# Order of VectorE's sums in the MLP chunks, and activation parts in halves at a layer's last down chunk, in a one-core fp32 encoder trunk

## The chip, the core and the metric

The kernel runs on one core of a Trainium2 chip. TensorE (PE in the profile, PEld for its weight loads) multiplies, VectorE (DVE) and ScalarE (ACT) make its operands and empty its banks, GpSimd (POOL) and SyncE (SP) issue DMAs. The metric is the device time of one execution in microseconds (us). Three runs of the kernel before gave 1590.45 to 1590.70 us, median 1590.61.

## The reference, cut to what matters

Two request groups of 512 and 256 tokens go through two layers, 768 tokens side by side in the kernel. The part that the change touches is the MLP that ends each layer's mixer:

```python
h = rms_norm(x, norm_mlp[i])
x = x + jnp.square(jax.nn.relu(h @ mlp_w_up[i])) @ mlp_w_down[i]     # 1024 -> 4096 -> 1024
gate = jax.nn.sigmoid(rms_norm(x, norm_ple[i]) @ ple_w_gate[i])
x = x + (p[i] @ ple_w_proj[i]) * gate
```

All of it is fp32.

## The kernel before, in words

**A product in three matmuls.** An fp32 value is split into a high part that TensorE takes at its faster fp32 rate (`hi`, written by an ACT copy) and the rest (`lo = value - hi`, a DVE subtraction, in some places a POOL DMA that adds). A product is hi·hi + hi·lo + lo·hi, so TensorE needs the `hi` part of a weight first and its `lo` part some matmuls later. `split` is `high` and then `low`.

**Seven products for eight.** Both MLP matrices are multiplied by a Strassen-Winograd scheme: a chunk of weights and of activations is cut in 2 x 2 blocks, and seven products of sums of blocks replace eight. The weight sums are made on the fly on DVE: `sums32` (line 479 and 480) gives the blocks s3 and s2, `sums14` (lines 484 and 485) gives s1 and s4. The activation sums are `t13` and `t42` (lines 408 to 414), and their high and low parts are written at lines 418 and 424; the parts of the activation blocks that enter directly are written at lines 450 and 454 (high) and 460 and 463 (low). All matmuls are issued at line 180.

**Jobs.** Each layer's MLP has 16 up chunks (u = 0 to 15; the first two are done plainly, without the scheme) and 8 groups of two down chunks. After the plain ones the order is: up 2g+2, down (g, 0), down (g, 1), up 2g+3, for g = 0 to 6, and then the last group's two down chunks, `down_first` and `down_last`. A job has seven products of 12 matmuls of 384 columns each. An even up chunk is thus followed by a down chunk; an odd one by an even up chunk or, for u = 15, called `final`, by `down_first`.

**What sets the order.** In this stage the instruction streams of ACT, PE and DVE run as the program writes them; each engine takes its instructions strictly in that order and waits at the first that isn't ready. While TensorE does one job, ACT and DVE prepare the weights of the next job (`v`, a `Weights7`), finish the job before (`pend`, a list of steps of which `late()` takes the next), and read the banks.

**An up chunk** (`up`, line 1355 on) issues for TensorE: w11 into bank `a`; s3 into `b`; s2 onto `a`; w12 onto `c`; s1 onto `a`; w22 onto `d`; s4 onto `a`. In between ACT copies `a` to `c` (line 1366), `b` to `p` (1373) and `a` to `d` (1378). The sum `a + p` is taken by DVE at line 1389, when s1 is done, and s4 may write `a` only after it has been read. On DVE there follow the rectified block from `c` (line 1146), the low part of the next direct weights (`wlo`, line 532), a `late()` step, the low part of s32 (`zlo`), `d + p` (line 1405, when w22 is done), and the rectified rest. Ahead of line 1389 DVE does `sums32`, `sums14` and one `late()` step (a `t` low part, line 424).

**A down chunk** begins with w11 into two banks `a`, then s3 into two banks of tag `B`, which has two banks in all: the second of them is the one that held the up chunk's `d`.

**The layer's end.** The last group's activations of u = 15 can't be prepared during other up or down chunks: they are needed at once. `up` with `final` prepares block x11; `down_first` waits for the rest: after its first product, ACT squares y2 (768 columns, line 1149), writes the high part of x21 and x22 (line 454), then copies both banks `a` to `C` (line 1452), then squares the rest of y1 (line 1518). `t13`, `t42` and the parts follow, 768 columns each. The last product block of u = 15 enters each of the w12 and s3 products late (`late=True`: first the matmuls with u = 14's activations). Then come the high and low parts of the sum weights s14 (`whi<-sum`, `wlo<-sum`).

Of the kernel before, what the change touches and what calls it, by code (L numbers as in the profile page):

```python
# [11 lines left out]
F32 = mybir.dt.float32  # L12
F32R = mybir.dt.float32r
AF = mybir.ActivationFunctionType
ALU = mybir.AluOpType
# [7 lines left out]
T = sum(SEQS)  # L23
# [14 lines left out]
H = T // 2  # L38
# [10 lines left out]
def trunk_kernel(ctx: ExitStack, tc: tile.TileContext, a: dict, out: bass.AP):  # L49
    nc = tc.nc  # L50
    act, dve, pe = nc.scalar, nc.vector, nc.tensor
# [75 lines left out]
    def bank(tag, name):  # L127
        pool = pair_of_banks if tag == "B" else psum
        return pool.tile([P, 512], F32, tag=tag, name=name, bufs=BANKS[tag])
# [72 lines left out]
    def slot(i, name, dt=F32R, n=T):  # L202

        return (slots if i < 32 else more).tile([P, n], dt, tag=f"S{i}", name=name)

    def big(name, dt=F32):

        nonlocal turn
        if more is None:
            return tmp.tile([P, T], dt, tag="t", name=name)  # L210
        turn += 1
        return tmp.tile([P, T], dt, tag=f"q{turn % 6}", name=name, bufs=1)
# [12 lines left out]
    class Norm:  # L225


        n = T
# [166 lines left out]
    class Sums:  # L395
# [30 lines left out]
        def added(self, i):  # L426

            hi, lo = self.t[i]
            act.activation(lo[:], hi[:].bitcast(F32), AF.Copy, scale=-1.0)
            nc.gpsimd.dma_start(lo[:], (self.q1, self.q2)[i][:], accum_op=ALU.add)  # L430
# [11 lines left out]
    class Acts(Sums):  # L442
# [14 lines left out]
        def lowx(self, i):  # L457
            if i == 0:
                hi, lo = self.x1
                dve.tensor_tensor(lo, self.q1[:, :H], hi.bitcast(F32), ALU.subtract)  # L460
            else:
                hi, lo = self.x2
                dve.tensor_tensor(lo[:], self.q2[:], hi[:].bitcast(F32), ALU.subtract)  # L463

    class Weights7:

# [80 lines left out]
    def product7(ps, w, key, xs, start, step=P, col=0):  # L547

        hi, lo = w.w[key]
        rhs = xs[QS7[key]]  # L550
        ks = [(slice(step * i + col, step * i + col + P), rhs[i]) for i in range(512 // step)]
        terms = [(hi[:, c], p) for c, ps_ in ks for p in ps_] + [(lo[:, c], ps_[0]) for c, ps_ in ks]
        for i, (a, b) in enumerate(terms):
            matmul(ps, a, b, start=start and i == 0, stop=i == len(terms) - 1, skip_group_check=True)
# [581 lines left out]
    def mlp(l, norm, nxt, w, places, early, product=None, begun=None, more_gates=()):  # L1136
# [8 lines left out]
        def rectified(t, src, o, e, op):  # L1145
            dve.scalar_tensor_tensor(t[:, o:e], src, 0.0, r[:, o:e], op, ALU.mult)

        def squared(t):
            act.activation(t[:], t[:], AF.Square)  # L1149

        def acts_of(u, y1, y2, rest):

            e = chunk_acts(u, y1, y2)
            return [
                lambda: squared(rest),
                lambda: e.highx(0),
                lambda: (e.highx(1), e.lowx(0), e.lowx(1), e.t13()),
                e.t42,
                lambda: e.high(0),
                lambda: e.high(1),  # L1160
                lambda: e.low(0),
                lambda: e.low(1),
            ]

        def chunk_acts(u, y1, y2):
            return Acts(y1, y2, places[7 * (u % 2) : 7 * (u % 2) + 7], groups[u // 2], u % 2)

        def late(n=1):

            for _ in range(n):  # L1170
                if pend:
                    pend.pop(0)()
# [182 lines left out]
        def up(u, w, make):  # L1355


            first, final = u == PLAIN[l], u == 2 * NG - 1
            w.low("s32")
            w.split("s14")  # L1360
            v = make()
            seven = isinstance(v, Weights7)
            a = bank("A", "a")[:, :H]
            product7(a, w, "w11", xs, True)
            c = bank("A" if first else "C", "c")[:, :H]
            act.activation(c, a, AF.Copy)
            late(len(pend) - 5)
            w.split("w22")
            late()
            b = bank("A" if first else "B", "b")[:, :H]  # L1370
            product7(b, w, "s3", xs, True)
            p = big("p")[:, :H]
            act.activation(p, b, AF.Copy)
            if seven:
                v.sums32()
            product7(a, w, "s2", xs, False)
            d = bank("B", "d")[:, :H]
            act.activation(d, a, AF.Copy)
            late(2)
            if seven:  # L1380
                v.sums14()
                (v.sum_added if final else lambda: v.high("s32"))()
            late()
            product7(c, w, "w12", xs, False)
            if seven:
                v.high("direct")
            product7(a, w, "s1", xs, False)
            y1, y2 = big("y1"), big("y2")
            dve.tensor_tensor(y2[:, H:], a, p, ALU.add)  # L1389
            rectified(y1, c, 0, H, ALU.max)  # L1390
            if final:
                e = chunk_acts(u, y1, y2)
                act.activation(y1[:, :H], y1[:, :H], AF.Square)
                e.highx(0)
            if seven:
                v.low("direct")
            late()
            if seven:
                v.low("s32")
            if final:  # L1400
                e.lowx(0)
            product7(d, w, "w22", xs, False)
            if seven:
                v.added("w22")
            dve.tensor_tensor(y2[:, :H], d, p, ALU.add)
            rectified(y2, y2[:], 0, T, ALU.min)
            if final:
                squared(y2)
                e.highx(1)
            product7(a, w, "s4", xs, False)  # L1410
            rectified(y1, a, H, T, ALU.max)
            if final:
                aside.append(e)
            else:
                pend.extend([lambda: squared(y2)] + acts_of(u, y1, y2, y1))
            return v

        def down(g, h, w, make):
# [58 lines left out]
            if end:  # L1477
                return (down_first, down_last)[h](w, before or make, top, low, products, copies, added, third, less)
# [31 lines left out]
        def down_first(w, make, top, low, products, copies, added, third, less):  # L1510


            e = aside.pop()
            a = [bank("A", "a")[:, :H] for _ in range(2)]
            products(a, "w11", True)
            e.lowx(1)
            c = copies("C", a)
            act.activation(e.q1[:, H:], e.q1[:, H:], AF.Square)
            e.t13()
            e.high(0)  # L1520
            e.t42()
            products(c, "w12", False, True)
            e.low(0)
            e.high(1)
            e.low(1)
            w.split("s14")
            v = make()
            p = third()
            added(top, 0, c, ALU.add)
            products(a, "s2", False)  # L1530
            d = copies("B", a)
            v.sums32()
            v.high("direct")
            v.sums14()
            v.high("s32")
            products(a, "s1", False)
            added(low, H, a, ALU.subtract)
            v.low("direct")
            products(d, "w22", False)
            v.added("w22")  # L1540
            added(low, 0, d, ALU.subtract)
            products(a, "s4", False)

            def rest():
                added(top, H, a, ALU.add)
                v.low("s32")
                v.low("s14")
                less(p)

            return v, (lambda: v.high("s14"), rest)  # L1550
# [69 lines left out]
        with tc.manual_schedule(engines={ET.Activation, ET.PE, ET.DVE}):  # L1620
            for i, (job, *args) in enumerate(jobs):

                def make():

                    what, *n = jobs[i + 1]
                    if what is not down:
                        return up_chunk(l, *n)
                    k = (KB // 2) * n[0] + 2 * n[1]
                    return Weights7(a_down[k], a_down[k + 1])

                a_down = a["down"][l]
                w = job(*args, w, make)
# [557 lines left out]
    others = [i for i in rest + old if i not in parts]  # L2190
# [120 lines left out]
```

## Time and profile before

| what | value |
|---|---|
| median of three runs | 1590.61 us (1590.45 to 1590.70) |
| profiled execution, its own time | 1591.22 us |
| its span, first to last instruction | 1589.4 us |
| granted TensorE clock, mean | 0.994 |
| MLP of layer 0 and of layer 1, in the span | about 290 to 748 us and 1042 to 1505 us |
| time from an even chunk's s4 to the next one's | 55.55 to 55.57 us |

A row of the timeline gives the start, the duration, the engine, the line, the operation, the tile written and those read, the shapes and the count of instructions merged into it; in square brackets, how long the engine was idle before it and what released it. Two DVE instructions overlap a little: the second starts before the recorded end of the first.

### The profile page before, as it was taken

To read this page: it belongs to the slowest core of one execution; us is meant where nothing else is said; L and a number is where in the kernel's file an instruction comes from. 1 tells how busy PE (TensorE), PEld (TensorE's weight loads), DVE (VectorE), ACT (ScalarE), POOL (GpSimd) and SP (SyncE) were. 2 spreads that over 40 slices of the span, in tenths; PEclk is the share of its full clock that TensorE was granted. 3 is DMA by queue.
4 is the path that set the end of the run, shared out by engine and by line. 5 is a ranking of instruction groups with operands and counts; after the bars stand their busy time and mean duration, and the time that the engine had idled before them with its cause. 6 is when DMAs were issued, how large, how long until landed. Compare 5 with 4: busy or idle time off the path is not lost.

```text
span 1589.4 us, 24597 instructions
## 1 busy us (share of the span) xinstructions
PE 1543.9 (97%) x9375; PEld 1489.7 (94%) x9375; DVE 1357.7 (85%) x2244; ACT 982.2 (62%) x1566; POOL 151.0 (9%) x172
## 2 busy tenths in 40 slices
PE   9999999999999999999989999999999999999996
PEld 7988889999999999999989999999999999999885
DVE  7599898898889889889898887869888988988986
ACT  7478766876566656667755344556656665665754
POOL 0211000011111111110000000000111111111000
PEclk9999999999999999999999999999999999999998
DMA  8854412445654644556522212122564554456522
GB/s 278 216 135 134 132 52 91 128 100 129 137 120 120 140 115 105 129 137 152 147 60 80 80 67 85 63 78 69 138 137 114 128 139 102 108 137 140 138 78 103
DMA packets 72694, 188.39 MB, mean 119 GB/s; under 512 B 8144, under 2 KB 26064, under 8 KB 72576
## 3 DMA queue, kind: packets, MB, share of 16 engines
q1 hardware_dynamic: 45440, 139.89, 28.3%
q0 software_dynamic: 27136, 46.93, 16.7%
q8 instruction: 73, 1.20, 0.3%
q14 instruction: 45, 0.37, 0.1%
HBM read 143.02 MB, written 10.48 MB: 97 GB/s over the span
## 4 chain that ended last, share of the span: by engine, by line
PE 61%; DVE 22%; ACT 10%; issue 4%; DMA 4%; SPq 0%; DVEq 0%; ACTq 0%
PE a L180 28%; PE mm L180 7%; PE b L180 6%; PE B L180 4%; PE C L180 4%; PE c L180 3%; PE d L180 2%; DVE t L424 2%; PE pt L847 1%; ACT y L1149 1%; PE gate L180 1%; PE p L180 1%; DVE act L463 1%; DVE pr L1689 1%; PE O L857 1%
## 5 line engine op out<-in xcount | busy, mean ns | idle before, releaser
L180 PE MATMUL a<-xs,whi 128*128 128x384 f32 x624 | 116.0, 329 | 11.2 <-DVE y L1389 9.9
L180 PEld LDWEIGHTS a<-xs,whi 128*128 128x128 f32 x624 | 102.5, 189 | 16.4 <-DVE y L1389 13.8
L180 PE MATMUL a<-t,zhi 128*128 128x384 f32 x568 | 109.5, 326 | 0.0
L180 PE MATMUL a<-t,whi 128*128 128x384 f32 x568 | 109.3, 326 | 0.0
L180 PE MATMUL b<-t,zhi 128*128 128x384 f32 x552 | 106.7, 326 | 0.3 <-DVE t L424 0.3
L180 PE MATMUL a<-act,whi 128*128 128x384 f32 x512 | 104.3, 326 | 0.0
L1475 POOL DMA_DIRECT2D x<-p x56 | 68.0, 1215 | 367.2 <-DVE x L1457 216.0
L504 ACT ACTIVATE whi<-sum 128x1024 fp32r<-128x1024 f32 x71 | 74.9, 1055 | 41.9 <-PE a L180 39.1
L532 DVE TENSOR_TENSOR wlo<-wraw,whi 128x1024 fp32r<-128x1024 f32 x74 | 90.1, 1218 | 10.9 <-ACT whi L504 10.9
L180 PEld LDWEIGHTS a<-t,whi 128*128 128x128 f32 x568 | 94.9, 189 | 0.6 <-ACT d L1565 0.6
L180 PEld LDWEIGHTS a<-t,zhi 128*128 128x128 f32 x568 | 95.1, 189 | 0.4 <-DVE t L424 0.4
L180 PEld LDWEIGHTS b<-t,zhi 128*128 128x128 f32 x552 | 92.3, 189 | 0.9 <-DVE t L424 0.9
L504 ACT ACTIVATE vhi<-wraw 128x512 fp32r<-128x512 f32 x71 | 44.4, 625 | 75.3 <-PE B L180 64.3
L504 ACT ACTIVATE zhi<-sum 128x1024 fp32r<-128x1024 f32 x71 | 74.8, 1054 | 22.2 <-DVE sum L480 22.2
L532 DVE TENSOR_TENSOR wlo<-sum,whi 128x1024 fp32r<-128x1024 f32 x71 | 86.5, 1218 | 2.2 <-ACT whi L504 2.2
L1457 DVE TENSOR_TENSOR x<-x,a 128x384 f32<-128x384 f32 x128 | 67.3, 549 | 23.6 <-PE a L180 11.8
L180 PEld LDWEIGHTS a<-act,whi 128*128 128x128 f32 x512 | 86.6, 189 | 0.3
L532 DVE TENSOR_TENSOR zlo<-sum,zhi 128x1024 fp32r<-128x1024 f32 x69 | 84.0, 1217 | 0.0
L504 ACT ACTIVATE whi<-wraw 128x1024 fp32r<-128x1024 f32 x76 | 79.4, 1045 | 1.9
L180 PE MATMUL mm<-xs_mix,whi 128*128 128x512 f32 (+1 forms) x320 | 77.3, 331 | 0.4 <-DVE pjs L610 0.4
L418 ACT ACTIVATE t<-y 128x768 fp32r<-128x768 f32 x64 | 52.3, 838 | 22.9 <-DVE y L409 17.3
L1457 DVE TENSOR_TENSOR x<-x,C 128x384 f32<-128x384 f32 x64 | 35.1, 553 | 35.3 <-PE C L180 29.2
(336 smaller groups left out, 4424.7 us busy)
## 6 DMA issues: line engine op xcount, KB each, us to landing
wraw<-in_up SPq DMA_DIRECT2D x64, 512.0 KB, 4.8
wraw<-in_down SPq DMA_DIRECT2D x64, 512.0 KB, 4.9
x<-p POOLq DMA_DIRECT2D x56, 384.0 KB, 6.4
wraw<-in_w_in SPq DMA_DIRECT2D x24, 512.0 KB, 3.5
vlo<-in_down POOLq DMA_DIRECT2D x32, 256.0 KB, 7.5
wraw<-in_gate SPq DMA_DIRECT2D x16, 512.0 KB, 4.1
vlo<-in_up POOLq DMA_DIRECT2D x28, 256.0 KB, 7.3
pj<-pjs SPq DMA_DIRECT2D x16, 384.0 KB, 2.8
```

What stands on the lines that cost most here:

```text
L180: pe.matmul(ps, lhsT=w, rhs=rhs, **flags)
L418: act.activation(t[0][:], (self.q1, self.q2)[i][:], AF.Copy)
L424: dve.tensor_tensor(lo[:], (self.q1, self.q2)[i][:], hi[:].bitcast(F32), ALU.subtract)
L463: dve.tensor_tensor(lo[:], self.q2[:], hi[:].bitcast(F32), ALU.subtract)
L504: act.activation(hi[:], src, AF.Copy)
L532: dve.tensor_tensor(lo[:], src, hi[:].bitcast(F32), ALU.subtract)
L847: pe.transpose(pt[:, h * P : (h + 1) * P], lg[h // 2][:, h % 2, b * P : (b + 1) * P], ident[:],)
L857: pe.matmul(O[:], lhsT=v, rhs=ph[:], start=b == 0, stop=False)
L1149: act.activation(t[:], t[:], AF.Square)
L1457: dve.tensor_tensor(t[:, o : o + H], t[:, o : o + H], f, op)
L1475: nc.gpsimd.dma_start(pairs[2 * h + 1][:, :, o : o + H], q, accum_op=ALU.add)
L1689: dve.tensor_tensor(q, q, natural(t[:, o:e]), ALU.mult)
```

## The change

Two things, in the functions above.

In an even up chunk (`soon` is 0), `sums14` and the `late()` step behind it are moved from ahead of `a + p` to right behind it. The odd chunks keep their order. The sum `a + p` is thus ahead of the next weights' other sums.

At the layer's end, the square and the high part of y2 leave `up`, and y2 is rectified in two halves. In `down_first`, the high part of the s14 weights comes first of all (its low part, behind s3), the two bank copies to `C` come as each bank is ready with the square of y2's first half between them, and the parts of the activations are written in halves of 384 columns (`part`, `tiles`), the half that TensorE needs next ahead of the others.

```diff
+        def part(self, t, i, j, low):
+            q, c = (self.q1, self.q2)[i], slice(H * j, H * j + H)
+            if low:
+                dve.tensor_tensor(t[1][:, c], q[:, c], t[0][:, c].bitcast(F32), ALU.subtract)
+            else:
+                act.activation(t[0][:, c], q[:, c], AF.Copy)
+
+        def tiles(self, at, names):
+            t = [slot(self.places[at + p], "t7") for p in range(2)]
+            self.keep(t, names)
+            return t
...
             late(2)
+            soon = u % 2
+
+            def others():
+                if seven:
+                    v.sums14()
+
+            if soon:
+                others()
             if seven:
-                v.sums14()
                 (v.sum_added if final else lambda: v.high("s32"))()
-            late()
+            if soon:
+                late()
             product7(c, w, "w12", xs, False)
             if seven:
                 v.high("direct")
             product7(a, w, "s1", xs, False)
             y1, y2 = big("y1"), big("y2")
             dve.tensor_tensor(y2[:, H:], a, p, ALU.add)
+            if not soon:
+                others()
+                late()
             rectified(y1, c, 0, H, ALU.max)
...
             dve.tensor_tensor(y2[:, :H], d, p, ALU.add)
-            rectified(y2, y2[:], 0, T, ALU.min)
-            if final:
-                squared(y2)
-                e.highx(1)
+            for o, n in ((0, H), (H, T)) if final else ((0, T),):
+                rectified(y2, y2[:, o:n], o, n, ALU.min)
...
             e = aside.pop()
+            w.high("s14")
             a = [bank("A", "a")[:, :H] for _ in range(2)]
             products(a, "w11", True)
-            e.lowx(1)
-            c = copies("C", a)
-            act.activation(e.q1[:, H:], e.q1[:, H:], AF.Square)
+            c = [bank("C", "c")[:, :H] for _ in range(2)]
+            act.activation(c[0], a[0], AF.Copy)
+            act.activation(e.q2[:, :H], e.q2[:, :H], AF.Square)
+            act.activation(c[1], a[1], AF.Copy)
+            x2 = e.tiles(5, ("x21", "x22"))
+            t13 = e.tiles(0, ("t1", "t3"))
+            t42 = e.tiles(2, ("t4", "t2"))
+            e.part(x2, 1, 0, False)
+            e.part(x2, 1, 0, True)
+            for q in (e.q1, e.q2):
+                act.activation(q[:, H:], q[:, H:], AF.Square)
             e.t13()
-            e.high(0)
+            e.part(x2, 1, 1, False)
+            e.part(t13, 0, 1, False)
+            products(c, "w12", False, True)
+            e.part(x2, 1, 1, True)
+            e.part(t13, 0, 1, True)
+            e.part(t13, 0, 0, False)
             e.t42()
-            products(c, "w12", False, True)
-            e.low(0)
-            e.high(1)
-            e.low(1)
-            w.split("s14")
+            e.part(t42, 1, 1, False)
+            e.part(t42, 1, 1, True)
+            e.part(t42, 1, 0, False)
+            e.part(t13, 0, 0, True)
+            e.part(t42, 1, 0, True)
             v = make()
             p = third()
+            w.low("s14")
             added(top, 0, c, ALU.add)
             products(a, "s2", False)
             d = copies("B", a)
```

## The prediction

> **What bounds the kernel now.** I read the page's busy times first, then the waits, one period of the MLP, and last the timeline of each engine by itself around an even up chunk and around a layer's end.
>
> ```profile
> PE 1543.9 (97%) x9375; PEld 1489.7 (94%) x9375; DVE 1357.7 (85%) x2244; ACT 982.2 (62%) x1566; POOL 151.0 (9%) x172
> ```
>
> TensorE is the bound: only a wait of its own, ended by another engine, can be won. The list of waits names one that belongs to the change (columns: total us, times, longest):
>
> ```profile
> PEld a L180 <- DVE y L1389: 13.8, 13, 1.9
> ```
>
> Line 1389 is `a + p`. It is waited for 13 times, once in each even up chunk but one: 1.9 us once and (13.8 - 1.9) / 12 = 0.99 us otherwise. One period of the MLP (columns: the stretch, its length, then each engine's busy time with its instructions):
>
> ```profile
> 395.99:451.54 55.55, 54.87 (x336) 54.57 (x336) 48.37 (x71) 34.16 (x50) 8.48 (x8) 1.00 0.54 124
> ```
>
> VectorE is idle for 55.55 - 48.37 = 7.2 us of it, so it isn't the clock over a period; it is only late at one place. VectorE alone there, from `sums32`'s second half to `d + p`:
>
> ```profile
> 392.70 0.69 DVE L480 TENSOR_TENSOR sum<-sum,wraw 128x512 f32<-128x512 f32 x1
> 393.31 0.68 DVE L484 TENSOR_TENSOR sum<-wraw 128x512 f32<-128x512 f32 x1
> 393.91 0.68 DVE L485 TENSOR_TENSOR sum<-wraw,sum 128x512 f32<-128x512 f32 x1
> 394.51 0.95 DVE L424 TENSOR_TENSOR t<-y,t 128x768 fp32r<-128x768 f32 x1
> 395.38 0.55 DVE L1389 TENSOR_TENSOR y<-a,p 128x384 f32<-128x384 f32 x1
> 395.85 0.55 DVE L1146 SCALAR_TENSOR_TENSOR y<-c,rstd_mlp 128x384 f32<-128x384 f32 x1
> 396.32 1.21 DVE L532 TENSOR_TENSOR wlo<-wraw,whi 128x1024 fp32r<-128x1024 f32 x1
> 397.45 0.95 DVE L424 TENSOR_TENSOR t<-y,t 128x768 fp32r<-128x768 f32 x1
> 398.32 1.22 DVE L532 TENSOR_TENSOR zlo<-sum,zhi 128x1024 fp32r<-128x1024 f32 x1
> 399.45 0.55 DVE L1405 TENSOR_TENSOR y<-d,p 128x384 f32<-128x384 f32 x1
> ```
>
> The rows stand back to back: starts lie 0.60 to 0.61 us apart behind a half sum, 0.87 behind a 768-column and 0.47 behind a 384-column operation, less than the durations, since two overlap. TensorE's side, the last matmuls of s1 and then the weight loads:
>
> ```profile
> 392.53 0.81 PE L180 MATMUL a<-t,wlo 128*128 128x384 f32 x4
> ```
>
> ```profile
> 393.02 1.33 PEld L180 LDWEIGHTS d<-t,vhi 128*128 128x128 f32 x8
> ...
> 395.99 1.27 PEld L180 LDWEIGHTS a<-xs,whi 128*128 128x128 f32 x8 [0.99 <-DVE y L1389]
> ...
> 398.53 0.35 PEld L180 LDWEIGHTS a<-act,wlo 128*128 128x128 f32 x2
> ...
> 400.81 0.68 PEld L180 LDWEIGHTS b<-t,zhi 128*128 128x128 f32 x4
> ```
>
> Undisturbed loads follow each other at 0.1625 us (eight end at +1.33 with the last lasting 0.19), so a product of twelve takes 1.95, and four jobs of seven products take 54.6 us. The period is 0.95 longer, and all of that is this wait: s4's first load was due at 393.02 + 1.95 = 394.97 and came at 395.99. (1.02 at the load costs 0.95: the first matmul catches up about 0.07.) s1 was ready at 392.53 + 0.81 = 393.34; `a + p` started 2.0 us later because `sums14` and a `late()` step stood ahead of it.
>
> **Even chunks, step by step.** Nothing is added or removed; three DVE instructions (0.60 + 0.60 + 0.87 = 2.07 us) go from ahead of `a + p` to behind it. No ACT, PE or DMA instruction moves. How soon VectorE sees the end of a product shows where it waits for one, in a down chunk:
>
> ```profile
> 696.98 0.49 PE L180 MATMUL C<-act,wlo 128*128 128x384 f32 x2
> ```
>
> ```profile
> 697.57 0.55 DVE L1457 TENSOR_TENSOR x<-x,C 128x384 f32<-128x384 f32 x1 [0.42 <-PE C L180]
> ```
>
> 0.10 us after 697.47. So `a + p` can start when its slot in the queue comes, 393.31, or 0.10 after s1's end: 393.44. It ends at 393.99, nearly 1.0 before s4's load is due. So this wait goes, and TensorE is 0.95 us earlier from there.
>
> What is late next? Everything behind `a + p` on VectorE keeps its place in time but for the 0.13 us it now waits for s1: same instructions, same sum. For TensorE, 0.95 earlier, three of them matter:
> - `wlo`: ends 396.32 + 1.21 + 0.13 = 397.66. The down chunk's first load of it, 398.53, is now due at 397.57. With 0.06 from DVE's end to the load (395.93 to 395.99 at s4) it comes at 397.72: 0.15 late, 0.08 after the catch-up.
> - `zlo`: ends 399.67 by the same sum; it adds about 0.06.
> - `d + p`: ends 399.45 + 0.55 + 0.13 = 400.13 and frees the second `B` bank, into which the loads at 400.81 lead. They are due at 400.81 - 0.95 + 0.14 = 400.00 and come at 400.19: 0.13 more.
>
> Together 0.27 of the 0.95 comes back, 0.68 is won. The delayed `sums14` itself has cover: the weights made of it are used by s1, behind four products (7.8 us) of the next job. `zhi` (ACT) waits only for `sums32`, which stays in place. SP's next fetches wait for the raw weights that `wlo` frees, 0.13 later; nothing of 0.13 us is at stake there. VectorE is then about 0.8 us further behind TensorE than now, and has the 7.2 us of idle time in the rest of the period to work that off.
>
> Twelve ordinary chunks give 12 x 0.68 = 8.2. The 1.9 us chunk is layer 0's first: VectorE is later there, the same three steps hold TensorE up again, and only the slack that they had (0.7 to 0.8) is won: 0.7. The even chunk without a wait is layer 1's first:
>
> ```profile
> 1094.15 0.69 DVE L480 TENSOR_TENSOR sum<-sum,wraw 128x512 f32<-128x512 f32 x1
> ```
>
> ```profile
> 1097.46 1.54 PE L180 MATMUL a<-xs,whi 128*128 128x384 f32 x8
> ```
>
> Its s1 ended at 1097.46 - 1.95 + 0.16 = 1095.67, so the moved `a + p` keeps VectorE waiting from 1094.76 to 1095.77, and all behind it comes 1.0 later. It then stands as the ordinary chunks will, and loses their 0.2 to 0.3. Even chunks in all: 8.2 + 0.7 - 0.2 = 8.7 us. Bounds: 13.3 if no other wait follows (12 x 0.95 + 1.85), 0 if the three steps give it all back.
>
> **The layer's end, step by step** (layer 0; layer 1 is the same 757 us later). ScalarE, then TensorE's first product of `down_first` and its loads, then VectorE:
>
> ```profile
> 718.73 0.84 ACT L1149 ACTIVATE y<-y 128x768 f32<-128x768 f32 x1 [1.74 <-DVE y L1146]
> 719.61 0.84 ACT L454 ACTIVATE act<-y 128x768 fp32r<-128x768 f32 x1
> 720.36 0.85 ACT L1452 ACTIVATE C<-a 128x384 f32<-128x384 f32 x2
> 721.13 0.51 ACT L1518 ACTIVATE y<-y 128x384 f32<-128x384 f32 x1
> ```
>
> ```profile
> 717.56 0.49 PE L180 MATMUL a<-act,wlo 128*128 128x384 f32 x2
> 717.89 0.81 PE L180 MATMUL a<-act,whi 128*128 128x384 f32 x4
> 718.54 0.49 PE L180 MATMUL a<-act,wlo 128*128 128x384 f32 x2
> ```
>
> ```profile
> 720.88 0.67 PEld L180 LDWEIGHTS C<-act,whi 128*128 128x128 f32 x4 [2.15 <-ACT C L1452]
> ...
> 731.24 0.68 PEld L180 LDWEIGHTS a<-act,whi 128*128 128x128 f32 x4
> ```
>
> ```profile
> 718.62 0.55 DVE L1146 SCALAR_TENSOR_TENSOR y<-a,rstd_mlp 128x384 f32<-128x384 f32 x1
> ...
> 725.87 1.23 DVE L532 TENSOR_TENSOR wlo<-sum,whi 128x1024 fp32r<-128x1024 f32 x1
> ...
> 730.47 1.01 DVE L1457 TENSOR_TENSOR x<-x,a 128x384 f32<-128x384 f32 x2
> ```
>
> The high part of s14, about 1.05 on ACT, falls into the 1.74 us in which ACT waits: free. The first bank is ready at 718.05 and is copied at once; y2's first half is squared (0.51); the second bank, ready at 719.03, is copied by 719.54. TensorE's 2.15 us wait shrinks to about 0.5. Then the chain alternates between ACT (0.51 a half) and DVE (0.47 a half, 0.59 where one needs the last): x21's parts to 720.5, the two squares to 720.84, `t13` 720.5 to 721.6, x22 low, t3 high 722.2, t3 low, `t42` 722.7 to 723.85, t2 high and low to 724.4, then t1, t4 and the s14 low part at 725.25. That is 0.62 ahead of 725.87, though TensorE by itself would be 2.15 - 0.5 = 1.6 ahead. From the s14 low part to `x<-x,a` VectorE is busy without a gap, 4.60 us, in both orders, and s4's load at 731.24 needs the first of these two sums; so VectorE decides: first sum 729.85 to 730.40, load at 730.46, 0.78 won. Six halves for three wholes cost VectorE 6 x 0.47 - 3 x 0.87 = 0.2, which is in the times above.
>
> [...]
>
> Behind it `down_last` and the gates are paced by TensorE and shift along. Two layers: 1.6 us. Bounds: -0.3 a layer if the halves only lengthen the chain, 1.6 a layer if VectorE doesn't decide.
>
> **The sum.** 1591.22 - 8.7 - 1.6 = 1580.9 against the profiled execution's own time (span 1589.4), which lies 0.61 above the median of the runs; for the median 1580.3.
>
> **Rivals.**
> - *Full release.* The three steps that I call late are in time, and VectorE isn't last at the layer's end: 13.3 + 2 x 1.6 = 16.5 won, 1574.1. For it: my 0.27 is made of margins of 0.1 to 0.2. Against: all three margins would have to be wrong by over 0.1 in one direction. 0.08.
> - *The wait moves.* `wlo` or the `B` bank is needed a few matmuls earlier than I read, or VectorE's lag isn't worked off in the down chunk and comes back at its sums: 0.3 a chunk is left, 13 x 0.3 + 0.6 = 4.5, 1586.1. Against: 7.2 us of idle time a period. 0.11.
> - *The order on VectorE isn't what the text says*: `a + p` stays where it was, only the ends gain: 1589. 0.04.
> - *Slower: `a + p` holds the queue.* VectorE now stands at `a + p` until s1 ends, with `sums14`, `wlo` and `zlo` queued behind. It decides from the point where that wait exceeds the slack of `wlo`, 398.53 - 397.59 = 0.94. Layer 1's first chunk shows such a wait, 1.0. If every chunk had it on top of today's lateness, TensorE would lose 1.0 at `wlo` for 0.68 won: 13 x 0.32 = 4.2 lost, 1594.8 with the ends unchanged. Against: in ordinary chunks VectorE reaches its slot at 393.31, 0.13 before s1 can be used. 0.04.
>
> **How the numbers follow.** My forecast has 0.73, with 1577 to 1584 as its own range. A measurement of this kernel can tell 0.2%, 3.2 us, from no change. Faster by more: the forecast, full release and most of the moved wait, 0.88; same 0.08; slower 0.04. The range goes from 1576.0, on the way to full release, to 1585.5, near the moved wait; it leaves out about 2 in 10.
>
> **What would show it.** Right: no wait of TensorE on line 1389 in even chunks; the period 54.8 to 55.0 instead of 55.55; small waits, 0.1 to 0.2, on `wlo`, `zlo` and line 1405; in layer 1's first chunk VectorE idle about 1.0 before line 1389; TensorE's wait for `C` about 0.5; a wait of s4 on line 1457 in `down_first`. Wrong: a period of 54.6 (nothing is late next), or a wait of 0.6 and more on one of the three; or a DVE queue that is later at the s14 low part than before.

## The result and the profile after

Four runs of the changed kernel took 1576.94 to 1580.24 us, median 1578.35; four of the kernel before on the same chip 1590.45 to 1590.83, median 1590.65. The ratio is 0.9923, 95% interval 0.9906 to 0.9941: faster by 0.8%, more than the 0.2% that the prediction set as its bound. The forecast was 1580.3 in 1576.0 to 1585.5. The profiled execution after took 1580.24 us (span 1578.5), 10.98 less than the profiled one before.

The page's busy times:

```profile
PE 1545.1 (98%) x9375; PEld 1488.0 (94%) x9375; DVE 1356.9 (86%) x2252; ACT 983.5 (62%) x1574; POOL 150.9 (10%) x172
```

The work is the same but for eight instructions more on VectorE and eight on ScalarE, the halves of two layers; busy times moved by 1.7 us at most (the weight loads). What went is waiting. From TensorE's list of waits, in the middle of layer 0's MLP (total us, times, longest):

```profile
PEld b L180 <- DVE y L1430: 1.0, 6, 0.2
PEld a L180 <- DVE x L1480: 0.7, 1, 0.7
PEld c L180 <- ACT c L1543: 0.5, 1, 0.5
PEld a L180 <- DVE t L469: 0.4, 1, 0.4
PEld a L180 <- ACT t L471: 0.3, 1, 0.3
...
```

`a + p`, now line 1411, isn't in it; in the whole kernel one wait of 0.22 on it is left, in layer 0's first even chunk, where it was 1.89. In its place stands `d + p` (1430), 0.17 us in each even chunk. At the layer's end there is 0.5 on `c` instead of 2.15 and a new wait of 0.7 on the sums of line 1480. One period, with the columns as before:

```profile
393.57:448.46 54.89, 54.89 (x337) 54.51 (x337) 48.29 (x71) 34.17 (x51) 8.48 (x8) 1.00 0.55 125
```

It was 55.55. VectorE in the even chunk, where `sums14` is lines 498 and 499:

```profile
391.32 0.69 DVE L494 TENSOR_TENSOR sum<-sum,wraw 128x512 f32<-128x512 f32 x1
392.04 0.56 DVE L1411 TENSOR_TENSOR y<-a,p 128x384 f32<-128x384 f32 x1
392.51 0.68 DVE L498 TENSOR_TENSOR sum<-wraw 128x512 f32<-128x512 f32 x1
393.11 0.68 DVE L499 TENSOR_TENSOR sum<-wraw,sum 128x512 f32<-128x512 f32 x1
393.71 0.95 DVE L424 TENSOR_TENSOR t<-y,t 128x768 fp32r<-128x768 f32 x1
...
395.05 1.22 DVE L546 TENSOR_TENSOR wlo<-wraw,whi 128x1024 fp32r<-128x1024 f32 x1
396.18 0.95 DVE L424 TENSOR_TENSOR t<-y,t 128x768 fp32r<-128x768 f32 x1
397.05 1.22 DVE L546 TENSOR_TENSOR zlo<-sum,zhi 128x1024 fp32r<-128x1024 f32 x1
398.19 0.55 DVE L1430 TENSOR_TENSOR y<-d,p 128x384 f32<-128x384 f32 x1
```

and TensorE beside it, first the end of s1, then the loads:

```profile
391.13 0.81 PE L180 MATMUL a<-t,wlo 128*128 128x384 f32 x4
```

```profile
392.92 0.68 PEld L180 LDWEIGHTS d<-t,vlo 128*128 128x128 f32 x4
393.57 1.33 PEld L180 LDWEIGHTS a<-xs,whi 128*128 128x128 f32 x8
...
395.52 0.68 PEld L180 LDWEIGHTS a<-act,whi 128*128 128x128 f32 x4
396.32 0.30 PEld L180 LDWEIGHTS a<-act,wlo 128*128 128x128 f32 x2
...
397.57 0.68 PEld L180 LDWEIGHTS b<-t,zhi 128*128 128x128 f32 x4
398.32 0.30 PEld L180 LDWEIGHTS b<-t,zlo 128*128 128x128 f32 x2
398.79 0.62 PEld L180 LDWEIGHTS b<-t,zhi 128*128 128x128 f32 x4 [0.17 <-DVE y L1430]
```

s1 ends at 391.94 and `a + p` starts at 392.04, 0.10 later. s4's first load follows at once. Then the three forecast delays can be counted off at 0.1625 us a load: `wlo` due at 395.52 + 4 x 0.1625 = 396.17, come at 396.32 (0.15); `zlo` due at 398.22, come at 398.32 (0.10); the second `B` bank due at 398.64, come at 398.79 (0.15). The first two have no bracket in the view: here they are seen only by such counting.

At the layer's end, ScalarE, then TensorE's loads, then VectorE:

```profile
711.48 1.04 ACT L518 ACTIVATE whi<-sum 128x1024 fp32r<-128x1024 f32 x1
712.65 0.47 ACT L1541 ACTIVATE c<-a 128x384 f32<-128x384 f32 x1
...
713.62 0.47 ACT L1543 ACTIVATE c<-a 128x384 f32<-128x384 f32 x1
```

```profile
714.15 0.30 PEld L180 LDWEIGHTS c<-act,whi 128*128 128x128 f32 x2 [0.53 <-ACT c L1543]
...
725.07 0.30 PEld L180 LDWEIGHTS a<-act,whi 128*128 128x128 f32 x2 [0.67 <-DVE x L1480]
```

```profile
714.55 0.56 DVE L469 TENSOR_TENSOR t<-y,t 128x384 fp32r<-128x384 f32 x1 [0.76 <-ACT t L471]
...
719.88 1.22 DVE L546 TENSOR_TENSOR wlo<-sum,whi 128x1024 fp32r<-128x1024 f32 x1
...
724.47 1.01 DVE L1480 TENSOR_TENSOR x<-x,a 128x384 f32<-128x384 f32 x2
```

Counted from the last up chunk's s4 load (714.69 before, 709.26 after), s14's low part starts at 10.62 instead of 11.18, and s4's load of `down_first` comes at 15.81 instead of 16.55. From there to the first load of the gates it is 16.06 instead of 16.11.

How much faster TensorE takes the split parts than whole fp32 values shows near the end of the same trace, at 256 columns each:

```profile
1561.80 2.17 PE L180 MATMUL gate<-xs_ple,gw 128*128 128x256 f32 x18
...
1564.48 0.60 PE L1998 MATMUL ss<-acc_final,ones 128*128 128x256 f32 x2
```

The matmuls on parts follow each other at 0.11 us; a sum of squares on whole values is two records, 0.22 apart.

### The profile page after: what moved, and what is told of

Its sections match the earlier page's. It is cut to its first block, busy times and chain, and to the rows that moved or that the text cites. A ratio compares the mean times of both kernels' runs of the same rounds, so it can differ in the third digit from the quotient of the medians.

```text
span 1578.5 us, 24629 instructions
## 1 busy us (share of the span) xinstructions
PE 1545.1 (98%) x9375; PEld 1488.0 (94%) x9375; DVE 1356.9 (86%) x2252; ACT 983.5 (62%) x1574; POOL 150.9 (10%) x172
## 4 chain that ended last, share of the span: by engine, by line
PE 71%; DVE 17%; ACT 7%; issue 3%; DMA 2%; SPq 0%; DVEq 0%; ACTq 0%
PE a L180 32%; PE mm L180 9%; PE b L180 8%; PE c L180 5%; PE d L180 4%; PE C L180 4%; PE B L180 4%; PE pt L861 1%; DVE pr L1727 1%; PE vp L180 1%; PE p L180 1%; PE O L871 1%; DVE wlo L546 1%; ACT L L848 1%; DVE y L2047 1%
## 5 line engine op out<-in xcount | busy, mean ns | idle before, releaser
L180 PE MATMUL a<-t,whi 128*128 128x384 f32 x584 | 113.3, 326 | 0.0
L1480 DVE TENSOR_TENSOR x<-x,a 128x384 f32<-128x384 f32 x128 | 67.4, 550 | 21.5 <-PE a L180 12.4
L180 PE MATMUL a<-t,wlo 128*128 128x384 f32 x292 | 65.6, 326 | 0.0
L180 PE MATMUL c<-xs,whi 128*128 128x384 f32 x336 | 64.0, 330 | 0.0
```

Of the source, the lines that this page charges most:

```text
L180: pe.matmul(ps, lhsT=w, rhs=rhs, **flags)
L1480: dve.tensor_tensor(t[:, o : o + H], t[:, o : o + H], f, op)
```

## The experiments

The theory is the prediction's: TensorE wins what it waited for `a + p`, gives back 0.27 a chunk at three later steps of the same VectorE queue, and the layer's end is won by the early copies and the halves. The rivals are its full release, its moved wait, and `a + p` holding up the queue. Diffs are against the changed kernel unless said otherwise. Four kernels ran beside each other on one chip, four on a second, two on a third, each time beside the kernel before. "End" below is the time from the last up chunk's s4 load to the s4 load of `down_first`, layer 0.

### The same kernel again, and each part alone

`after_again` is the changed kernel.

> The changed kernel once more, to see how far its runs lie apart and where. First theory (a + p ahead lets s4 start on time; VectorE's next steps give back 0.24 us a period): a period of 54.89 us again, and the spread of 3.3 us between its first four runs comes from outside the MLP, from transfers in the stage before. Rival: the spread comes from the periods themselves, with a period nearer 54.6 us in the faster runs. Median 1578 to 1579 us.

1578.97 us (1578.66 to 1580.22), ratio 0.9927 [0.9912, 0.9941]; period 54.89, end 15.82. The two profiled executions of this kernel have the same periods, so the 0.7 us between their spans (1578.5 and 1577.8) lie elsewhere. No execution of it under 1578 us was profiled, so where the faster ones win isn't shown.

The even chunks alone, against the kernel before:

```diff
+            soon = u % 2
...
+            if soon:
+                others()
             if seven:
-                v.sums14()
                 (v.sum_added if final else lambda: v.high("s32"))()
-            late()
+            if soon:
+                late()
...
             dve.tensor_tensor(y2[:, H:], a, p, ALU.add)
+            if not soon:
+                others()
+                late()
```

> Only a + p ahead in the even chunks; the layer's end as before. First theory: the even chunks carry nearly all of it, 8.7 to 10 us won, 1580.6 to 1582 us; period 54.89 us; TensorE's 2.15 us wait for the banks C is back at both layer ends. Rival (the layer's end carries more than I reckoned, because the earlier part lets later stages start sooner): less than 7 us won, 1584 us or more.

1581.12 us (1579.41 to 1581.73), ratio 0.9937 [0.9924, 0.9950]; period 54.89, end 16.54.

The layer's end alone: the changed kernel with the order of the even chunks as before.

```diff
-            soon = u % 2
...
             if seven:
+                v.sums14()
                 (v.sum_added if final else lambda: v.high("s32"))()
-            if soon:
-                late()
+            late()
...
-            if not soon:
-                others()
-                late()
```

> Only the layer's end changed; the even chunks as before. First theory: 0.8 us a layer, 1.6 us in all, 1589.0 us; period 55.55 us, s4 of down_first waits 0.7 us for VectorE's sums. Rival (VectorE doesn't decide there): 3.2 us, 1587.4 us. Second rival (halves cost more than they bring): 1590.6 us or more.

1587.34 us (1585.04 to 1589.38), ratio 0.9979 [0.9970, 0.9989]; period 55.57, end 15.81.

Each part does in the trace what it does in the whole, to 0.03 us, and nothing of the other's. The two gains, 9.3 and 3.1 by medians, add up to 12.4 (11.5 for the whole on that chip). The end's 3.1 is more than its two places show, 2 x (16.55 - 15.81 + 0.05) = 1.6; its interval reaches from 1.7 to 4.8 us. Where the rest comes from isn't shown. The stretch from layer 0's gates to the first even chunk's s4 in layer 1's MLP, nearly all of which the change doesn't touch, was 349.2 us in that profile and 350.1 in the one before. In the profiles of this study that stretch varied by 1.0 us, the tail behind layer 1's gates by 2.7 and the start of layer 0's MLP by 2.3. So a period is read to 0.02, a whole run to a microsecond or two.

### Is VectorE's queue behind `a + p` what decides now?

`sums14` is made twice over behind `a + p` in even chunks, with the same values: 1.2 us of VectorE that nothing waits for.

```diff
             if not soon:
                 others()
+                if seven:
+                    v.sums14()
                 late()
```

> The changed kernel with sums14 made twice behind a + p in every even chunk, 1.2 us more on VectorE there (two starts 0.60 apart, twice). First theory: what is behind a + p on VectorE is what TensorE waits for next, so all of it is paid: period 54.89 + 1.2 = 56.1 us, 14 x 1.2 = 16.8 us over the changed kernel, 1595 us, slower than the kernel before. Rival (TensorE is the bound again and VectorE's steps lie in cover): no more than 3 us over the changed kernel, 1581 us.

1597.02 us (1594.0 to 1598.31), ratio 1.0036 [1.0025, 1.0048]; its own span 1592.2. TensorE's waits and one period:

```profile
PEld a L180 <- DVE wlo L546: 19.5, 14, 2.3
```

```profile
394.21:450.31 56.10, 55.07 (x338) 54.52 (x338) 49.52 (x73) 34.18 (x51) 8.48 (x8) 1.00 0.52 123
```

54.89 became 56.10: the two additions, 0.60 each, are paid in full, at `wlo`, with VectorE idle for 56.10 - 49.52 = 6.6 us of the period. That idle time lies elsewhere in it. The slower rival's mechanism is real and its price is one to one (1.21 us a period for 1.20); the change stays clear of it because VectorE reaches `a + p` only 0.11 us before it can be done, so that what stands behind comes 0.11 later than before; VectorE's idle time over a period is no protection.

### Which of the moved steps costs the 0.3 that came back?

`sums_only` moves `sums14` alone; the `late()` step stays ahead of `a + p`.

```diff
-            if soon:
-                late()
+            late()
             product7(c, w, "w12", xs, False)
...
             if not soon:
                 others()
-                late()
```

> As the changed kernel, but only sums14 goes behind a + p; the late step (0.87 us) stays ahead of it. First theory (only VectorE's order counts, and a + p has 1 us to spare): a + p ends 0.2 us before s4 is due, so s4 still starts on time; VectorE no longer stands 0.13 us at a + p, so the steps behind come 0.13 earlier: period 54.75 us instead of 54.89, 1.7 us less in all, not told from the changed kernel by its time. Rival (each step ahead of a + p costs in proportion): 0.87 of the 2.07 us moved back, period about 55.2 us, 4 us more.

1578.29 us (1576.89 to 1579.06), ratio 0.9922 [0.9908, 0.9935]; period 54.78. VectorE, then TensorE's waits in layer 0:

```profile
393.68 0.95 DVE L424 TENSOR_TENSOR t<-y,t 128x768 fp32r<-128x768 f32 x1
394.55 0.55 DVE L1410 TENSOR_TENSOR y<-a,p 128x384 f32<-128x384 f32 x1
```

```profile
PEld b L180 <- DVE y L1428: 1.2, 7, 0.2
PEld a L180 <- DVE y L1410: 1.1, 1, 1.1
...
```

`a + p` ends at 395.10, and s4's load comes at 395.32 without a wait. VectorE no longer stands 0.11 us at `a + p` until s1 ends, so that all behind it is 0.11 earlier: 54.78 against 54.89. Only layer 0's first chunk waits for `a + p`, once, 1.1. The step that mattered is `sums14`; the moved `late()` cost a little.

`low_behind` puts the second `late()` step, which stood between `wlo` and `zlo`, behind `d + p` in even chunks:

```diff
-            late()
+            if soon:
+                late()
             if seven:
                 v.low("s32")
...
             dve.tensor_tensor(y2[:, :H], d, p, ALU.add)
+            if not soon:
+                late()
```

> As the changed kernel, but in even chunks the second late step (the low part of t4 and t2, 0.87 us), which stands between wlo and zlo, goes behind d + p. First theory (the 0.24 us left in a period are waits for wlo, zlo and the bank that d + p frees): zlo and d + p come 0.87 earlier, their waits go, only that for wlo stays, 0.08: period 54.68 us, 14 x 0.2 = 2.8 us less. Rival (something else holds TensorE, as the second bank B itself): 54.89 us again.

1577.07 us (1576.96 to 1578.14), ratio 0.9915 [0.9901, 0.9928]; period 54.69. TensorE's loads in the same place:

```profile
396.62 0.30 PEld L180 LDWEIGHTS a<-act,wlo 128*128 128x128 f32 x2
...
397.86 0.68 PEld L180 LDWEIGHTS b<-t,zhi 128*128 128x128 f32 x4
398.51 0.35 PEld L180 LDWEIGHTS b<-t,zlo 128*128 128x128 f32 x2
398.84 0.68 PEld L180 LDWEIGHTS b<-t,zhi 128*128 128x128 f32 x4
```

`zlo` and the `B` bank are in time; only `wlo` is late. That splits what came back: 54.89 - 54.69 = 0.20 belongs to `zlo` and `d + p`, and 54.69 - 54.60 = 0.09 to `wlo`.

### What decides at the layer's end?

`end_adds` takes `sums14` of `down_last`'s weights out of the way of the sums that s4 waits for:

```diff
-            v.sums14()
             v.high("s32")
             products(a, "s1", False)
             added(low, H, a, ALU.subtract)
+            v.sums14()
```

> As the changed kernel, but in down_first sums14 goes behind the two sums of line 1480 that read a. First theory (VectorE decides at the layer's end, s4 waits 0.67 us for the first of these sums): that wait goes, 0.6 us a layer, from the final chunk's s4 to down_first's 15.2 instead of 15.8 us, 1.2 us in all. Rival (another wait takes its place in down_last, where sums14's parts are then late): no change from the final chunk's s4 to the gates, 31.87 us.

1578.49 us (1577.97 to 1578.75), ratio 0.9924 [0.9910, 0.9937]; end 15.13, and 16.10 on to the gates. VectorE, then the loads:

```profile
723.24 0.69 DVE L494 TENSOR_TENSOR sum<-sum,wraw 128x512 f32<-128x512 f32 x1
723.85 1.01 DVE L1480 TENSOR_TENSOR x<-x,a 128x384 f32<-128x384 f32 x2
```

```profile
724.64 0.35 PEld L180 LDWEIGHTS B<-t,vlo 128*128 128x128 f32 x2
724.97 0.35 PEld L180 LDWEIGHTS a<-act,whi 128*128 128x128 f32 x2
```

The sum comes 1.2 earlier in the queue, s4 has no wait, and 0.68 is won (0.64 with the 0.04 lost on to the gates). So VectorE's queue did decide in the changed kernel, as forecast, and by 0.68 only: then s4's load follows the one ahead of it, and TensorE decides.

Two kernels, each run once (1581.11 and 1580.49 us, the kernel before beside them 1590.57) and read from the profile of that run, ask which edit at the layer's end brought the 0.74. `whole_parts` keeps the early s14 and the copies as they come, but writes the parts in whole tiles, and squares y2 whole:

```diff
-            act.activation(e.q2[:, :H], e.q2[:, :H], AF.Square)
+            act.activation(e.q2[:], e.q2[:], AF.Square)
...
-            e.part(x2, 1, 0, False)
-            e.part(x2, 1, 0, True)
-            for q in (e.q1, e.q2):
-                act.activation(q[:, H:], q[:, H:], AF.Square)
...
+            whole(x2, e.q2, False)
+            act.activation(e.q1[:, H:], e.q1[:, H:], AF.Square)
+            whole(x2, e.q2, True)
...
```

> The changed kernel, but with the activations' parts of a layer's last down chunk in whole tiles of 768 columns again; the copies of C as they come and the early high part of s14 stay. Read from the last chunk's s4 to the last chunk's own s4 load on a (16.55 us before, 15.81 after). My theory: the gain comes from the order, since the high part of s14 no longer stands behind the parts on ScalarE; two halves take VectorE some 0.07 us more than a whole, so the low part of s14 comes only about 0.2 us later here: about 16.0. Rival, as the prediction has it: the halves carry most of it, because a whole part of 0.95 us holds VectorE up ahead of the low part of s14: 16.4 to 16.55. From s4 to the gates 16.05 in both.

End 16.54 in layer 0 and 16.56 in layer 1, against 16.55 before: the whole gain is gone. VectorE at the start of the parts, and TensorE's waits from 713 to 727 us:

```profile
715.22 0.96 DVE L1550 TENSOR_TENSOR t<-y,t 128x768 fp32r<-128x768 f32 x1 [1.58 <-ACT t L1552]
```

```profile
PEld c L180 <- ACT c L1543: 1.0, 1, 1.0
PEld b L180 <- ACT t L1552: 0.7, 1, 0.7
PEld b L180 <- DVE t L1550: 0.6, 1, 0.6
PEld c L180 <- DVE t L1550: 0.4, 1, 0.4
PEld a L180 <- DVE t L1550: 0.2, 1, 0.2
```

The theory under test here was mine after the result, that the order does it and the halves are incidental; it fell. With whole tiles VectorE stands 1.58 us instead of 0.76 for the first high part, and TensorE, which waits for the parts themselves, loses 2.9 us in five places where the changed kernel loses 0.53 + 0.41 + 0.35 = 1.3, and 0.67 more at s4's wait for the sum. Half a microsecond of it is the wait for `c` (1.02 instead of 0.53), behind the square of the whole of y2; so it is the halves of the square and of the parts together that this kernel tests. s4 then comes without a wait: TensorE is the later of the two, and VectorE's queue doesn't matter.

`late_high` keeps the halves and puts the high part of s14 back behind them:

```diff
             e = aside.pop()
-            w.high("s14")
...
             e.part(t42, 1, 0, False)
+            w.high("s14")
             e.part(t13, 0, 0, True)
```

> The changed kernel, but with the high part of s14 put back behind the activations' parts on ScalarE; the copies of C as they come and the halves stay. From the last chunk's s4 to its s4 load on a (16.55 us before, 15.81 after). My theory: VectorE's low part of s14 waits for the high part only some 0.15 us more than it waits for its own queue, since the halves set ScalarE free early enough: about 15.95. Rival: the low part stands behind the last high part and the whole gain is lost: 16.4 to 16.55. From s4 to the gates 16.05 in both.

End 15.92 and 15.94. Of the 0.74, the early s14 brings 0.11 in layer 0 (0.15 in layer 1): with it put back, ScalarE's copies to `B` come later and hold TensorE for 0.65, and s4 waits for VectorE's sum for 0.17 only. The rest needs the halves. What the bank copies that come as each bank is ready bring by themselves was not tested: both kernels keep them.

### The version that follows

`all_in_cover` has `low_behind` and `end_adds`, and in even chunks `sums14` goes behind `wlo`, in the slot that the second `late()` left:

```diff
             if not soon:
-                others()
                 late()
...
-            late()
+            if soon:
+                late()
+            else:
+                others()
...
             dve.tensor_tensor(y2[:, :H], d, p, ALU.add)
+            if not soon:
+                late()
...
```

> Both of these, and sums14 of the even chunks behind wlo as well, so that nothing TensorE waits for stands behind it. First theory: period 54.60 us, TensorE's own; 14 x 0.29 + 1.2 = 5.3 us less than the changed kernel, 1573.5 us. Rival (sums14 is then late for ScalarE, whose next instruction, the high part of s14, stands ahead of the bank copies): ScalarE's copies come over 1 us late, TensorE waits for a bank, no gain or a loss.

1575.76 us (1573.57 to 1577.26), ratio 0.9906 [0.9892, 0.9919], the lowest median of the study, though its interval overlaps that of the changed kernel (0.9906 to 0.9941): by the time alone the two aren't told apart, and what it wins is read from the traces. Period and TensorE's waits in the middle of layer 0's MLP:

```profile
394.62:449.22 54.60, 54.60 (x338) 54.60 (x337) 48.20 (x71) 33.96 (x51) 8.48 (x8) 1.00 0.55 126
```

```profile
PEld c L180 <- ACT c L1547: 0.5, 1, 0.5
PEld a L180 <- DVE t L469: 0.4, 1, 0.4
PEld a L180 <- ACT t L471: 0.3, 1, 0.3
...
```

The list has no wait for `d + p` but one of 0.2 in layer 0's first even chunk, and none for `wlo` or the sums of line 1480. In the period TensorE's loads are busy for all of the 54.60 us: nothing is left there for an order of VectorE to win. Against the changed kernel this is 0.29 a period by the trace, 12 times, 0.5 and 0.3 in the layers' first even chunks, and 0.64 at each layer's end: 5.5 in all. The profiled spans differ by 1578.5 - 1573.7 = 4.8, because other stages lie differently: layer 0's MLP was reached 1.5 us later in this profile, and the stretch from its gates to layer 1's first even chunk took 0.7 less.

## Why the prediction was right

**The wait on `a + p`.** Forecast: gone, `a + p` at 0.10 behind s1's end, 0.13 later than its slot. Measured: gone, 0.10, and 0.11. One is left against the forecast, 0.22 in layer 0's first chunk, where VectorE itself is later: `a + p` ends at 337.71 and s4's load follows at 337.76. Shown by the trace, and by `end_only`, which has the wait (55.57) when the order is undone.

**What comes back.** Forecast 0.08 (`wlo`) + 0.06 (`zlo`) + 0.13 (`B` bank) = 0.27, leaving 0.68 of 0.95. Measured: 0.15 late at `wlo` as forecast, worth 0.09; the other two 0.20 against 0.19. The period fell by 0.66 to 54.89, in the middle of the forecast 54.8 to 55.0. This is the step on which the number hung, and it came from adding the same 0.13 us to rows of the trace before.

**The special chunks.** Layer 0's first: counted from the start of its second half of `sums32` to the next up chunk's s4 load, 381.32 - 337.14 = 44.18 before and 379.92 - 336.55 = 43.37 after, 0.8 won for a forecast of 0.7 (`end_only` 44.19, `even_only` 43.38). Its new wait is `wlo`, 1.10, since VectorE is later there. In layer 1's first chunk VectorE does stand at `a + p`, as forecast:

```profile
1089.67 0.56 DVE L1411 TENSOR_TENSOR y<-a,p 128x384 f32<-128x384 f32 x1 [0.94 <-PE a L180]
```

The prediction took this chunk for one without a wait before the change. The rows before, VectorE and then the loads, show a small one:

```profile
1096.83 0.55 DVE L1389 TENSOR_TENSOR y<-a,p 128x384 f32<-128x384 f32 x1
```

```profile
1096.65 0.68 PEld L180 LDWEIGHTS d<-t,vlo 128*128 128x128 f32 x4
1097.44 1.27 PEld L180 LDWEIGHTS a<-xs,whi 128*128 128x128 f32 x8
```

s4's load was due at 1096.65 + 4 x 0.1625 = 1097.30 and came at 1097.44, 0.06 behind the end of `a + p`: 0.14 late, without a bracket. From the `vlo` loads ahead of it to the next up chunk's s4 load, which has this wait in it, the chunk takes 1132.44 - 1090.54 = 41.90 after and 1138.33 - 1096.65 = 41.68 before: 0.22 lost where 0.2 was forecast.

**The layer's end.** Forecast: wait for C about 0.5, s14's low part 0.62 earlier, s4 waiting on VectorE's sums, 0.78 a layer. Measured: 0.53, 0.56, yes, 0.74 (0.79 up to the gates). `end_adds` shows that VectorE decides, `whole_parts` that the halves carry it. Before the change TensorE decided, by 0.16 us: its load at 731.24 followed the previous one, and the sum would have let it go at 731.08.

**The price of the halves.** The prediction charged them by the distance between starts, 0.47 us a half against 0.87 a whole tile, and not by the duration of one instruction (0.55 and 0.95 us in the rows). The changed kernel runs them so where nothing holds them:

```profile
718.46 1.50 DVE L469 TENSOR_TENSOR t<-y,t 128x384 fp32r<-128x384 f32 x3
```

Three halves take 1.50 = 2 x 0.47 + 0.56, and 0.79 a layer was won up to the gates for a forecast of 0.78. In `whole_parts` the fewer, larger instructions were slower by 0.73 at this place, where another engine waits for the first half.

**The sum.** 12 x 0.67 + 0.8 - 0.2 = 8.6 for the even chunks (forecast 8.7), 1.6 for the ends (1.6): 10.2 of the profiled executions' 10.98. The other 0.8 lies in stages that the change doesn't touch: VectorE reached layer 0's first even chunk 0.6 earlier (336.55 against 337.14), and the tail behind layer 1's gates was 0.3 shorter. Between the medians it is 12.3, 2 us more than the forecast has; where the further 1.3 lies isn't shown, since the faster executions weren't profiled. Stages outside the change vary by as much from profile to profile, and no experiment here ties them to the change.

**The rivals.** Full release is what `all_in_cover` has in the period; the changed kernel doesn't, because of the three steps. The moved wait would have shown as a period of about 55.25. That `a + p` stays where it was is refuted by the rows of VectorE, where it now stands ahead of line 498. The slower one needed some 1 us more behind `a + p`: `sums_twice` put it there and was slower than the kernel before.

## What to carry to other kernels

An engine that is idle for an eighth of a period (7.2 of 55.55 us here) can still be the one that decides at a single place: list what stands ahead of the operation that the bound engine waits for, move what nobody needs yet, and then carry the small delay on through the queue, row by row, to the next due times. When the first wait was gone, margins of 0.10 to 0.15 us decided here, and two of the three didn't appear as waits; they had to be counted from load to load. Split a tile where another engine waits for its first half, and judge it by that wait, not by the split engine's own sum.

## What the runs showed that was not expected

A wait of 1.02 us at a weight load cost 0.95, and one of 0.15 cost 0.09: the loads behind it stand closer and catch up some 0.06 (eight loads take 1.27 us behind a wait, 1.33 otherwise). The stages outside the change differed by up to 2.7 us between profiles of this study, more than the 1.6 us that the layer's end shows in its own places; the end alone measured 3.1 us.
